# A hybrid decoder layer: the first feed-forward product, nine feature groups token-major, with seven products for eight in half of their k

## The chip, the cores and the metric

The kernel runs on one core of one Trainium2 chip. The metric is device time of one execution in microseconds (us). The core has five instruction streams: TensorE (PE; its weight loads are listed as PEld), VectorE (DVE), ScalarE (ACT), GpSimd (POOL) and SyncE (SP), which issues the loads. Each engine takes its instructions in the order in which the program emits them and waits at those whose inputs or buffers aren't ready.

## The reference

One post-norm decoder layer over 256 tokens, D = 2048: a token-mixing part (attention, a gated MLP over tokens, a state-space branch, gates and an output product) and a feed-forward part of width D_FF = 5632. What the change touches is the feed-forward part:

```python
x = _layer_norm(ALPHA * x + merged @ w_o[l], ln1_g[l], ln1_b[l]).astype(dt)
gate_f, up = jnp.split(x @ w_ffn_in[l], 2, axis=-1)
f = (jax.nn.silu(gate_f) * up) @ w_ffn_out[l]
x = _layer_norm(ALPHA * x + f, ln2_g[l], ln2_b[l]).astype(dt)
```

## The kernel before

**Numbers in two parts.** Every product is made from float32 values split in two: a high part (the value rounded by the type fp32r, `split_h`, line 254, on ScalarE) and the remainder (value minus high part, `split_l`, line 265, on VectorE; both of its inputs lie in SBUF). A product a.b is taken as ah.bh + al.bh + ah.bl.

**Units.** The whole program is a list of units. A unit is one weight tile of up to 128 x 1024 values (512 KB): it is loaded into a `raw` tile (4 buffers), split into `wh` and `wl` (4 buffers each), and used by its matmuls. The main loop (line 1210) goes through the units in order. `advance` emits the loads and the splits of high parts ahead of the unit that is due, as far as the four buffers allow; `remainders` emits split_l after the unit's `post`, so the order of VectorE's work is: what `post` does, then the remainders of the units to come. `top_up` (line 285) emits a load when fewer than four raw tiles are loaded and not yet split. All loads go through SP's one queue.

**The first product, x @ w_ffn_in.** It has 88 feature tiles of 128: for each f of 44 a gate tile and an up tile, alternating (`f1`, line 1137). The first four go through `quad_tiles`, beside the end of the layer norm; the other 84 through `wide` (line 83). There the weights are stationary and the 256 tokens stream: `wide_mm` (line 74) takes for each of 16 k-tiles one matmul of 512 columns on line 79 (high part of the weights by high and low part of the activations, `x1T`, which holds [high | low] of the tokens, feature-major) and one of 256 columns on line 80 (remainder of the weights by the high part). A tile takes two units. `post_f1` (line 1040) adds the two halves of the PSUM bank, takes tanh of the gate, multiplies, and splits the product into `h_tile(f)`: h0 (tag x24) holds f 0 to 11, and eleven tiles of tag s6 hold three f each. h is the second product's activation, again feature-major.

**The second product, h @ w_ffn_out.** `tall` and `tall_mm` (lines 169 and 159) work the other way: a token tile's activations (128 x 128) are stationary and 512 output features stream, three matmuls for each k-tile and token tile on lines 165 to 167. The result is token-major. w_v, w_zv and w_o are made in this way too; w_o's activations, the tiles m, are of tag s6.

**Memory.** Tiles of one tag share a fixed number of buffers, laid out one tag after the other. The large tags are t32 (x1T), t16 (z, the residual stream after the first layer norm, until the second), raw, wh, wl, x24, s6 (11 buffers of 1536 values per partition) and the temporaries. After the constants, and between x24 and s6, stand small tiles whose sizes aren't multiples of 1 KB; one of them is `s5i`, 96 bytes, ahead of s6. PSUM has four banks of tag mm and four of tag sd.

**Elsewhere on GpSimd.** It runs the state-space recurrence (lines 544 to 547, 48 values a partition) in the first half of the program, adds gated branches (line 868) and a part of the layer norms (lines 937 and 938). In the first feed-forward product it does nothing.

Of the kernel before, what the change touches and what calls it, by code (L numbers as in the profile page):

```python
# [25 lines left out]
NJ = 24  # L26
# [6 lines left out]
def hybrid_layer(ctx: ExitStack, tc: tile.TileContext, d: dict, out: bass.AP):  # L33
# [5 lines left out]
    V, A, G, T = nc.vector, nc.scalar, nc.gpsimd, nc.tensor  # L39

    RAW_BUFS, HL_BUFS, AHEAD = 4, 4, 4

    def bank(tag="mm"):
        return psp.tile([128, 512], F32, tag=tag, bufs=4, name=f"ps_{tag}")

    def tmp(n=512):

        if n <= 256:
            t = sb.tile([128, 256], F32, tag="t1", bufs=6, name="tmp1")
        else:  # L50
            t = sb.tile([128, 512], F32, tag="t2", bufs=6, name="tmp2")
        return t[:, :n]

    def s6(shape, dt, name):
        return sb.tile(shape, dt, tag="s6", bufs=11, name=name)

    def copy_split(hi, lo, src, scale=1.0):
        A.activation(hi, src, AF.Copy, scale=scale)  # L58
        if scale == 1.0:
            V.tensor_tensor(lo, src, hi.bitcast(F32), op=ALU.subtract)  # L60
        else:
            V.scalar_tensor_tensor(lo, src, scale, hi.bitcast(F32), op0=ALU.mult, op1=ALU.subtract)


    class Unit:
        def __init__(self, src, k, n, mm, post=None, before=None, uses=1, home=None, fence=False):
            self.src, self.k, self.n = src, k, n
            self.mm, self.post, self.before = mm, post, before
            self.uses, self.home, self.fence = uses, home, fence

# [134 lines left out]
    def spawn(gen, rate=1, first=False):  # L205

        tasks.append((gen, rate, first))
        return gen
# [12 lines left out]
    def later(fn, wait=1):  # L221

        deferred.append([fn, wait])
# [16 lines left out]
    with tc.manual_schedule():  # L240
# [4 lines left out]
        def raw_tile():  # L245
            return sb.tile([128, 1024], F32, tag="raw", bufs=RAW_BUFS, name="raw")

        def load(n):
            u = units[n]
            r = raw_tile()  # L250
            nc.sync.dma_start(r[:, :u.k * u.n], u.src)
            raws[n] = r

        def split_h(n):
            u = units[n]
            m = u.k * u.n
# [5 lines left out]
            A.activation(h[:, :m], raws[n][:, :m], AF.Copy)  # L262
            hl[n] = rest[n] = (h, l)

        def split_l(n):
            m = units[n].k * units[n].n
            h, l = rest.pop(n)
            V.tensor_tensor(l[:, :m], raws.pop(n)[:, :m], h[:, :m].bitcast(F32), op=ALU.subtract)  # L268

        pos = {}  # L270

# [106 lines left out]

        def s5_setup():
            P = s5["P"]  # L380
            PI = sb.tile([128, NJ], I32, tag="s5i", bufs=1, name="s5i")
# [639 lines left out]
        def h_tile(f):  # L1021
            if f < 12:
                if f == 0:
                    big["h0"] = sb.tile([128, 12, 512], F32R, tag="x24", bufs=1, name="h0")
                return big["h0"][:, f, :]
            i = (f - 12) // 3
            if (f - 12) % 3 == 0 and ("h", i) not in big:
                big["h", i] = s6([128, 3, 512], F32R, f"h{i}")
            return big["h", i][:, (f - 12) % 3, :]

# [9 lines left out]
        def post_f1(f, up):  # L1040
# [11 lines left out]
                    copy_split(y[:, 0:256], y[:, 256:512], w, 0.5)  # L1052
            return post

        def post_f2(g):
# [19 lines left out]
        def ln2_load():  # L1075
            w = sb.tile([128, 2, D], F32, tag="t32", bufs=1, name="ln2w")
# [67 lines left out]
        for srcs, post in f1[4:]:  # L1144
            wide(srcs, 8, act_x1, post)
# [60 lines left out]
        pos.update(load=4, h=4, l=4, live=4, seq=seq)  # L1206
        while top_up():
            pass
        marks["s5"] = spawn(s5_setup())
# [140 lines left out]
```

## Time and profile before

| | us |
|---|---|
| median of 3 runs | 1604.29 (1601.53 to 1605.39) |
| the profiled execution | 1604.32 |
| its span, first to last instruction | 1602.6 |
| TensorE busy | 1580.8 (99%) |
| VectorE busy | 931.0 (58%) |
| ScalarE busy | 763.8 (48%) |
| GpSimd busy | 559.9 (35%) |
| mean granted TensorE clock | 0.995 |

The busy times are sums over the whole span. TensorE's matmuls are pipelined, so one instruction's listed duration is longer than the distance to the next; the work of a stretch is read from the number of matmuls in a window and its length. A line of a timeline gives start, duration, engine, line and operation, out<-in, shapes; a number in brackets at its end is idle time before it and what ended that.

### The profile page before, as it was taken

The numbers are of one execution on the slowest core, as the hardware profiler recorded it, in microseconds if no ns is written. First come the engines' busy times: TensorE is split into PE (matmuls) and PEld (weight loads), VectorE is DVE, ScalarE is ACT, GpSimd is POOL, SyncE is SP. The second block draws the span as 40 slices with busy tenths as digits, with TensorE's granted clock in tenths as the row PEclk, the third lists the DMA queues.
The fourth block names the chain that finished last, engine by engine and source line by source line (L and its number), as shares of the span: only waits on it lengthen the run. The fifth ranks groups of instructions, "written<-read, shape, count | busy, mean of one in ns | idle before, by whom it ended". The sixth has DMA issues, their size and how long they took to land.

```text
span 1602.6 us, 24113 instructions
## 1 busy us (share of the span) xinstructions
PE 1580.8 (99%) x9094; PEld 1366.3 (85%) x9094; DVE 931.0 (58%) x1232; ACT 763.8 (48%) x1040; POOL 559.9 (35%) x1147
## 2 busy tenths in 40 slices
PE   8999999999999999999999999999999999999996
PEld 7888888898999998889789888888888888888885
DVE  5444555556855565469667556565555555445455
ACT  5444434456544444475444545554444544333342
POOL 7569999933999999203011000000000000000002
PEclk9999999999999999999999999999999999999998
DMA  8575557655656555557863565555555556666663
GB/s 275 176 251 186 187 203 207 155 148 188 211 188 198 194 184 194 178 164 209 286 222 118 190 193 184 184 184 184 186 185 192 183 193 237 204 187 192 186 188 101
DMA packets 106492, 307.50 MB, mean 192 GB/s; under 512 B 27567, under 2 KB 28079, under 8 KB 106120
## 3 DMA queue, kind: packets, MB, share of 16 engines
q1 hardware_dynamic: 106280, 305.82, 59.7%
q8 instruction: 71, 1.16, 0.3%
q14 instruction: 45, 0.37, 0.1%
q0 software_dynamic: 96, 0.15, 0.0%
HBM read 303.78 MB, written 5.53 MB: 193 GB/s over the span
## 4 chain that ended last, share of the span: by engine, by line
PE 94%; DVE 3%; DMA 1%; ACT 1%; issue 0%; POOL 0%; SPq 0%; POOLq 0%; ACTq 0%
PE ps_mm L79 40%; PE ps_mm L80 20%; PE ps_mm L165 9%; PE ps_mm L166 9%; PE ps_mm L167 9%; DVE wl L268 1%; PE ps_mm L857 1%; PE ps_mm L858 1%; PE ps_mm L856 1%; PE ps_sd L522 1%; PE ps_sd L691 1%; PE ps_mm L108 0%; PE ps_mm L111 0%; PE ps_sd L670 0%; DMA ln<-in_ln_g_dram 0%
## 5 line engine op out<-in xcount | busy, mean ns | idle before, releaser
L268 DVE TENSOR_TENSOR wl<-raw,wh 128x1024 fp32r<-128x1024 f32 (+1 forms) x544 | 654.2, 1227 | 167.1 <-ACT wh L262 166.6
L262 ACT ACTIVATE wh<-raw 128x1024 fp32r<-128x1024 f32 (+1 forms) x544 | 556.7, 1024 | 369.1 <-PE ps_mm L167 171.6
L79 PE MATMUL ps_mm<-xT,wh 128*128 128x512 f32 x1344 | 480.6, 400 | 6.6 <-ACT wh L58 5.9
L79 PE MATMUL ps_mm<-x1T,wh 128*128 128x512 f32 x1344 | 474.9, 399 | 0.0
L80 PE MATMUL ps_mm<-xT,wl 128*128 128x256 f32 x1344 | 378.9, 282 | 0.5 <-DVE wl L268 0.5
L80 PE MATMUL ps_mm<-x1T,wl 128*128 128x256 f32 x1344 | 377.5, 281 | 0.0
L79 PEld LDWEIGHTS ps_mm<-xT,wh 128*128 128x128 f32 x1344 | 254.3, 189 | 67.1 <-ACT wh L58 5.9
L79 PEld LDWEIGHTS ps_mm<-x1T,wh 128*128 128x128 f32 x1344 | 252.6, 188 | 63.0
L937 POOL TENSOR_TENSOR z<-z,ln2w 128x512 f32<-128x512 f32 (+1 forms) x4 | 5.2, 1302 | 732.5 <-ACT z L936 732.5
L80 PEld LDWEIGHTS ps_mm<-xT,wl 128*128 128x128 f32 x1344 | 256.1, 191 | 1.5 <-DVE wl L268 0.8
L80 PEld LDWEIGHTS ps_mm<-x1T,wl 128*128 128x128 f32 x1344 | 253.9, 189 | 0.0
L546 POOL TENSOR_TENSOR X<-X,t 128x48 f32<-128x48 f32 x255 | 129.1, 506 | 48.6 <-ACT X L526 48.6
L544 POOL TENSOR_TENSOR t<-s5keep,X 128x48 f32<-128x48 f32 x254 | 126.6, 498 | 44.5 <-ACT X L526 24.7
L547 POOL TENSOR_TENSOR X<-X,t 128x48 f32<-128x48 f32 x255 | 129.9, 509 | 20.0
L166 PE MATMUL ps_mm<-wl,h 128*128 128x512 f32 x340 | 134.1, 394 | 0.0
L165 PE MATMUL ps_mm<-wh,h 128*128 128x512 f32 x340 | 134.1, 394 | 0.0
L167 PE MATMUL ps_mm<-wh,h 128*128 128x512 f32 x340 | 134.1, 394 | 0.0
L1037 DVE TENSOR_TENSOR tmp<-ps_mm,tmp 128x256 f32<-128x256 f32 x88 | 37.3, 424 | 152.9 <-ACT tmp L1036 152.9
L545 POOL TENSOR_TENSOR t<-s5keep,X 128x48 f32<-128x48 f32 x254 | 108.5, 427 | 0.0
L315 ACT ACTIVATE tmp<-ps_mm,bcol 128x256 f32<-128x256 f32 x90 | 42.7, 474 | 137.6 <-PE ps_mm L80 137.4
L1036 ACT ACTIVATE tmp<-ps_mm 128x256 f32<-128x256 f32 x88 | 33.8, 384 | 151.6 <-PE ps_mm L80 151.6
L165 PEld LDWEIGHTS ps_mm<-wh,h 128*128 128x128 f32 x340 | 64.0, 188 | 15.0
(214 smaller groups left out, 1775.6 us busy)
## 6 DMA issues: line engine op xcount, KB each, us to landing
raw<-in_w_f_dram SPq DMA_DIRECT2D x264, 512.0 KB, 4.3
raw<-in_w_b_dram SPq DMA_DIRECT2D x164, 512.0 KB, 4.6
raw<-in_w_o_dram SPq DMA_DIRECT2D x32, 512.0 KB, 5.0
raw<-in_w_v_dram SPq DMA_DIRECT2D x24, 512.0 KB, 4.0
raw<-in_w_p_dram SPq DMA_DIRECT2D x32, 384.0 KB, 3.4
raw<-in_w_zv_dram SPq DMA_DIRECT2D x16, 384.0 KB, 3.6
tmp<-tab SPq DMA_DIRECT2D x64, 64.0 KB, 3.2
raw<-in_w_p_dram SPq DMA_DIRECT2D x16, 256.0 KB, 2.9
```

The lines of the kernel that those rows point to most:

```text
L79: T.matmul(ps, lhsT=h[:, j * 128:(j + 1) * 128], rhs=a, start=k == 0, stop=last, skip_group_check=True)
L80: T.matmul(ps[:, 0:256], lhsT=l[:, j * 128:(j + 1) * 128], rhs=a[:, 0:256], start=False, stop=last, skip_group_check=True)
L165: T.matmul(ps[:, :n], lhsT=ah, rhs=hs, start=k == 0, stop=False)
L166: T.matmul(ps[:, :n], lhsT=ah, rhs=ls, start=False, stop=False)
L167: T.matmul(ps[:, :n], lhsT=al, rhs=hs, start=False, stop=k == total - 1)
L262: A.activation(h[:, :m], raws[n][:, :m], AF.Copy)
L268: V.tensor_tensor(l[:, :m], raws.pop(n)[:, :m], h[:, :m].bitcast(F32), op=ALU.subtract)
L315: A.activation(t, ps[:, 256:512], AF.Identity, bias=bcol[:, col:col + 1], scale=scale)
L544: G.tensor_tensor(t1, keep[:, 0], prev, op=ALU.mult)
L545: G.tensor_tensor(t2, keep[:, 1], prev[:, :, ::-1], op=ALU.mult)
L546: G.tensor_tensor(cur, cur, t1, op=ALU.add)
L547: G.tensor_tensor(cur, cur, t2, op=ALU.add)
```

## The change

1. **Groups.** The first 8 feature tiles (f 0 and 1 in the quad, f 2 and 3 wide) and the last 8 (f 40 to 43) stay as they were. The 72 tiles between become nine groups (`seven(g)`, g = 1 to 9) of four f, gate and up: per group two matrices of 512 columns, gate (`g`) and up (`u`). They are made token-major, like the second product: three matmuls of 512 columns for each k-tile, token tile and matrix (`three`).
2. **Seven products for eight.** For k-tiles 0 to 7, taken in pairs (SP = 4 steps), the 2 x 2 blocks (token tile by k-tile, k-tile by gate/up) are multiplied by Strassen's scheme in Winograd's form. The weights' combinations are made by GpSimd in `combine`, four subtractions or additions of 128 x 512 a step; one is made in place in the `u` tile before its split. Each step has four units: `g` and `u` (1024 values a partition), `t1` (512) and `tt` (1024); t1 and tt have no load and are split like the others. The activations' combinations are made once (`sums`: ten GpSimd operations) and split into `S`. For k-tiles 8 to 15 a group has eight plain units of 1024, two for each pair of k-tiles, that go on in the same PSUM banks.
3. **Results.** `evict` (after step 4) copies four PSUM banks on ScalarE and combines them on GpSimd (four operations of 128 x 512); `gates_` and `ups` add the other four banks on VectorE (one input in PSUM), take tanh and multiply (four operations with both inputs in SBUF, in `rest`). The result is token-major; `turns(g)` turns it with eight transposes of 128 x 128 during the next group and splits it into h.
4. **Loads.** A weight tile now takes two k-tiles of four feature tiles, so that its source is in pieces of 1 KB where it was 4 KB a partition. `g` tiles live in tag s6, three ahead (two in the last group); `top_up` counts raw and `g` tiles apart.
5. **z** goes to DRAM before the groups and comes back at the second product, since `S` takes its place (t16).
6. **Addresses.** `s5i` moves to the constants and 320 bytes of padding follow it; all large tiles then start at multiples of 1 KB.

```diff
+    PAD = 80
+    SP = 4
+    FIRST, LAST = 1, 9
...
         def load(n):
             u = units[n]
-            r = raw_tile()
-            nc.sync.dma_start(r[:, :u.k * u.n], u.src)
+            if u.role in ("t1", "tt"):
+                return
+            if u.role == "g":
+                r = u.pair["g"] = s6([128, 1536], F32, "gt")
+                pos["g"] += 1
+            else:
+                r = raw_tile()
+                pos["raw"] += 1
...
+            if u.role == "g":
+                combine(u.pair)
+            elif u.role == "t1":
+                raws[n] = u.pair["g"][:, 1024:1536]
+            elif u.role == "tt":
+                raws[n] = u.pair["t"]
             A.activation(h[:, :m], raws[n][:, :m], AF.Copy)
...
+        def combine(p):
+            p["t"] = s6([128, 1024], F32, "tt")
+            b = [p[e][:, 0:1024].rearrange("p (f k c) -> p k f c", f=4, k=2) for e in "gu"]
+            b11, b21, b12, b22 = b[0][:, 0], b[0][:, 1], b[1][:, 0], b[1][:, 1]
...
+            G.tensor_tensor(t1, b12, b11, op=ALU.subtract)
+            G.tensor_tensor(b12, b22, b12, op=ALU.subtract)
+            G.tensor_tensor(t2, b12, b11, op=ALU.add)
+            G.tensor_tensor(t4, b21, t2, op=ALU.subtract)
...
         def top_up():
             seq = pos["seq"]
-            if pos["load"] < len(seq) and pos["load"] - pos["l"] < RAW_BUFS:
+            if pos["load"] < len(seq):
+                u = units[seq[pos["load"]][0]]
+                if u.role == "g" and pos["g"] >= u.pair["ahead"] or u.role in (None, "u") and pos["raw"] >= RAW_BUFS:
+                    return False
...
+        s5["i"] = const.tile([128, NJ], I32, name="s5i")
+        const.tile([128, PAD], F32, name="pad")
...
+        def first_sums():
+            big["zd"] = dram.tile([128, 2, D], F32, name="zd")
+            for t in range(2):
+                nc.sync.dma_start(big["zd"][:, t, :], big["z"][:, t, :])
+            spawn(sums())
...
+        def three(ps, a, h, l, start, stop):
+            T.matmul(ps, lhsT=a[0], rhs=h, start=start, stop=False)
+            T.matmul(ps, lhsT=a[1], rhs=h, start=False, stop=False)
+            T.matmul(ps, lhsT=a[0], rhs=l, start=False, stop=stop)
...
+                    if role == "g":
+                        prod(1, act2(0, 2 * i), cols(h, 0), cols(l, 0), i)
+                        prod(2, act2(0, 2 * i + 1), cols(h, 1), cols(l, 1), i)
+                    elif role == "u":
+                        prod(7, act_s(2, i), cols(h, 0), cols(l, 0), i)
+                        prod(3, act_s(3, i), cols(h, 1), cols(l, 1), i)
+                    elif role == "t1":
+                        prod(5, act_s(0, i), h[:, 0:512], l[:, 0:512], i)
+                    else:
+                        prod(6, act_s(1, i), h[:, 0:512], l[:, 0:512], i)
+                        prod(4, act2(1, 2 * i + 1), h[:, 512:1024], l[:, 512:1024], i)
...
+            def evict():
+                c = P["c"] = {n: tmp() for n in (1, 7, 5, 6)}
+                for n in (1, 7, 5, 6):
+                    A.activation(c[n], P[n], AF.Copy)
+                G.tensor_tensor(c[6], c[1], c[6], op=ALU.add)
+                G.tensor_tensor(c[7], c[6], c[7], op=ALU.add)
+                G.tensor_tensor(c[6], c[6], c[5], op=ALU.add)
+                G.tensor_tensor(c[5], c[7], c[5], op=ALU.add)
...
+            def ups():
+                c = P["c"]
+                for n, m in ((6, 3), (5, 8)):
+                    V.tensor_tensor(c[n], P[m], c[n], op=ALU.add)
+                def rest(t):
+                    w, a, b = P["w"][t], c[(1, 7)[t]], c[(6, 5)[t]]
+                    V.scalar_tensor_tensor(w, w, 1.0, a, op0=ALU.add, op1=ALU.mult)
+                    V.tensor_tensor(w, w, b, op=ALU.mult)
...
+            src = [d["w_f1"][8 * g + up:8 * g + 8:2].rearrange("f p k c -> p f k c") for up in range(2)]
...
+        for g in range(FIRST, LAST + 1):
+            seven(g)
```

More of the change, by code (lines that the diff above doesn't have):

```diff
@@ L380, in s5_setup @@
             P = s5["P"]
-            PI = sb.tile([128, NJ], I32, tag="s5i", bufs=1, name="s5i")
+            PI = s5["i"]
             keep = const.tile([128, 3, NJ, 2], F32, name="s5keep")
@@ L1026, in h_tile @@
             i = (f - 12) // 3
-            if (f - 12) % 3 == 0 and ("h", i) not in big:
+            if ("h", i) not in big:
                 big["h", i] = s6([128, 3, 512], F32R, f"h{i}")
@@ L1053, in post_f1, with sums @@
             return post
+        def first_sums():
[3 more added lines that the diff above has]
+            spawn(sums())
+        def sums():
+            srs = []
+            for j in range(SP // 2):
+                xr = s6([128, 4, 256], F32, "xr")
+                x = big["x1T"][:, 4 * j:4 * j + 4, :].bitcast(F32)
+                G.tensor_tensor(xr, x[:, :, 0:256], x[:, :, 256:512], op=ALU.add)
+                sr = s6([128, 4, 2, 128], F32, "sr")
+                a = xr.rearrange("p (i k) (t c) -> p k t i c", k=2, t=2)
+                a11, a21, a12, a22 = a[:, 0, 0], a[:, 0, 1], a[:, 1, 0], a[:, 1, 1]
+                G.tensor_tensor(sr[:, 0], a21, a22, op=ALU.add)
+                G.tensor_tensor(sr[:, 1], sr[:, 0], a11, op=ALU.subtract)
+                G.tensor_tensor(sr[:, 2], a11, a21, op=ALU.subtract)
+                G.tensor_tensor(sr[:, 3], a12, sr[:, 1], op=ALU.subtract)
+                srs.append(sr)
+            for _ in range(3):
+                yield
+            big["S"] = sb.tile([128, 4, SP, 256], F32R, tag="t16", bufs=1, name="S")
+            for j in range(SP // 2):
+                o = big["S"][:, :, 2 * j:2 * j + 2, :]
+                for s in range(4):
+                    copy_split(o[:, s, :, 0:128], o[:, s, :, 128:256], srs[j][:, s])
+                    if s % 2:
+                        yield
@@ new lines, in seven, with cols, prod, mk @@
+        def seven(g):
+            P = {}
+            def cols(w, j):
+                return w.rearrange("p (f k c) -> p k f c", f=4, k=2)[:, j]
+            def prod(n, a, h, l, i):
+                if i == 0 and n not in P:
+                    P[n] = bank("sd" if n in (1, 5, 6, 7) else "mm")
+                three(P[n], a, h, l, i == 0, n in (1, 5, 6, 7) and i == SP - 1)
+            def mk(role, i):
+                def mm(h, l):
+                    if role == "g":
[9 more added lines that the diff above has]
+                        prod(4, act2(1, 2 * i + 1), h[:, 512:1024], l[:, 512:1024], i)
+                return mm
+            def mk8(up, i):
+                def mm(h, l):
+                    for t in range(2):
+                        n = ((2, 4), (3, 8))[up][t]
+                        if n == 8 and i == SP:
+                            P[8] = bank("mm")
+                        for j in range(2):
+                            three(P[n], act2(t, 2 * i + j), cols(h, j), cols(l, j),
+                                  n == 8 and (i, j) == (SP, 0), (i, j) == (7, 1))
+                return mm
+            def begin():
+                if g > FIRST:
+                    spawn(turns(g - 1))
+            def evict():
[6 more added lines that the diff above has]
+                G.tensor_tensor(c[5], c[7], c[5], op=ALU.add)
+            def gates_():
+                c = P["c"]
+                for n, m in ((1, 2), (7, 4)):
+                    V.tensor_tensor(c[n], P[m], c[n], op=ALU.add)
+                P["w"] = [tmp(), tmp()]
+                for t, n in enumerate((1, 7)):
+                    A.activation(P["w"][t], c[n], AF.Tanh, scale=0.5)
+            def ups():
+                c = P["c"]
+                for n, m in ((6, 3), (5, 8)):
+                    V.tensor_tensor(c[n], P[m], c[n], op=ALU.add)
+                def rest(t):
+                    w, a, b = P["w"][t], c[(1, 7)[t]], c[(6, 5)[t]]
+                    V.scalar_tensor_tensor(w, w, 1.0, a, op0=ALU.add, op1=ALU.mult)
+                    V.tensor_tensor(w, w, b, op=ALU.mult)
+                rest(0)
+                later(lambda: rest(1), 0)
+                big["w", g] = P["w"]
+            src = [d["w_f1"][8 * g + up:8 * g + 8:2].rearrange("f p k c -> p f k c") for up in range(2)]
+            for i in range(8):
+                s = [a[:, :, 2 * i:2 * i + 2, :].rearrange("p f k c -> p f (k c)") for a in src]
+                if i < SP:
+                    pair = {"ahead": 3 if g < 9 else 2}
+                    units.append(Unit(s[0], 8, 128, mk("g", i), role="g", pair=pair,
+                                      before=begin if i == 0 else None))
+                    units.append(Unit(s[1], 8, 128, mk("u", i), role="u", pair=pair))
+                    units.append(Unit(None, 4, 128, mk("t1", i), role="t1", pair=pair))
+                    units.append(Unit(None, 8, 128, mk("tt", i), role="tt", pair=pair,
+                                      post=evict if i == SP - 1 else None))
+                else:
+                    units.append(Unit(s[0], 8, 128, mk8(0, i), post=gates_ if i == 7 else None))
+                    units.append(Unit(s[1], 8, 128, mk8(1, i), post=ups if i == 7 else None))
@@ new lines, in turns @@
+        def turns(g):
+            tag = "mm" if g < LAST else "sd"
+            for _ in range(6 if g < LAST else 2):
+                yield
+            for t in range(2):
+                ps = bank(tag)
+                for f in range(4):
+                    T.transpose(ps[:, f * 128:(f + 1) * 128], big["w", g][t][:, f * 128:(f + 1) * 128], ident)
+                yield
+                f = 4 * g
+                while f < 4 * g + 4:
+                    n = min(4 * g + 4, 12 if f < 12 else f + 3 - f % 3) - f
+                    h_tile(f)
+                    y = big["h0"][:, f:f + n] if f < 12 else big["h", (f - 12) // 3][:, f % 3:f % 3 + n]
+                    copy_split(y[:, :, t * 128:(t + 1) * 128], y[:, :, 256 + t * 128:256 + (t + 1) * 128],
+                               ps.rearrange("p (f c) -> p f c", f=4)[:, f - 4 * g:f - 4 * g + n], 0.5)
+                    f += n
+                for _ in range(3 if g < LAST else 1):
+                    yield
@@ L1075, in ln2_load @@
         def ln2_load():
+            big["z"] = sb.tile([128, 2, D], F32, tag="t16", bufs=1, name="z")
+            for t in range(2):
+                nc.sync.dma_start(big["z"][:, t, :], big["zd"][:, t, :])
             w = sb.tile([128, 2, D], F32, tag="t32", bufs=1, name="ln2w")
@@ L1205, in hybrid_layer @@
             seq.insert(at + i, (first + i, at))
[L1206 removed]
+        pos.update(load=4, h=4, l=4, live=4, raw=0, g=0, seq=seq)
         while top_up():
```

34 lines of the change are left out of this document (30 added, 4 removed).

## The prediction

> **What bounds the kernel now.** I read the page first (busy times, then the chain that ended last), then a table by windows of the stretch that the change rewrites: the first feed-forward product after its quad, 84 feature tiles on lines 79 and 80. Columns of the window row: TensorE, its weight loads, VectorE, ScalarE, GpSimd, granted clock, DMA share, GB/s.
>
> ```profile
> PE 1580.8 (99%) x9094; PEld 1366.3 (85%) x9094; DVE 931.0 (58%) x1232; ACT 763.8 (48%) x1040; POOL 559.9 (35%) x1147
> ...
> PE 94%; DVE 3%; DMA 1%; ACT 1%; issue 0%; POOL 0%; SPq 0%; POOLq 0%; ACTq 0%
> ```
>
> ```profile
> 868.70:1343.30 474.60, 474.60 (x2689) 411.62 (x2688) 282.26 (x382) 238.17 (x340) 0.00 (x0) 1.00 0.58 187
> ```
>
> TensorE never stops there, at full clock; VectorE works 59% of the time, ScalarE 50%, GpSimd not at all. So TensorE sets the time: 474.6 / 84 = 5.65 us a tile, 45.2 us for the eight tiles of one group, 407 us for the nine groups. All sums below stand against the profiled execution, 1604.3 us (span 1602.6 and 1.7 around it), which is also the median.
>
> **TensorE's part.** The new form (a token tile's activations as weights, 512 weight columns streaming, three products) is that of the second product, lines 165 to 167. Two windows of its second pass, TensorE alone:
>
> ```profile
> 1404.93:1421.28 16.35, 16.35 (x73) 1.00 0.60 191
> 1421.28:1466.25 44.97, 44.97 (x193) 1.00 0.64 188
> ```
>
> The windows start and end on a product, so they hold 72 and 192: 0.227 and 0.234 us each. The 72 read h0, which starts at the same offset within 1 KB as the weight tiles; the 192 read tiles of tag s6, 96 bytes (the integer tile s5i) further on. The change puts all of them at multiples of 1 KB, so I take 0.227 for the groups and keep 0.234 as the other end. A group has 4 steps of seven products and 4 of eight, 60 triples, 180 instructions: 40.9 us (42.1). Turning the result back costs two sets of four transposes; one set is this row, at most 0.60:
>
> ```profile
> 839.53 0.60 PE L956 MATMUL ps_sd<-ident,z 128*128 128x128 f32 x4
> ```
>
> TensorE's group is then 42.1 us (43.3) for 45.2: 3.1 us saved, 28 us in nine groups, if TensorE still sets the time. Outside the groups, 32 of 44 k-tiles of the second product and all of w_o read s6 tiles: 768 + 384 products. If w_o's run like the 192, 0.007 us each give 8 us (0 if offsets don't matter).
>
> **What is added on the other engines.** Per group: ScalarE makes 20 high parts of 1024 and 4 of 512 where it made 16; by the 1058 ns of the row below and half of it, 23.3 us, and eight operations of 512 for the results, 4.2 us more: far below 42. VectorE makes as many remainders (split_l), GpSimd gets 16 combinations and 4 additions of 128x512. These two I price together, because the trace shows them waiting for each other:
>
> ```profile
> L268 DVE TENSOR_TENSOR wl<-raw,wh 128x1024 fp32r<-128x1024 f32 x474 | 583.9, 1255 | 163.2 <-ACT wh L262 162.7
> L262 ACT ACTIVATE wh<-raw 128x1024 fp32r<-128x1024 f32 x474 | 501.2, 1058 | 357.4 <-PE ps_mm L167 171.6 <-PE ps_mm L79 79.1 <-DMA raw<-in_w_o_dram 28.2
> ```
>
> ```profile
> 200.90 1.17 POOL L544 TENSOR_TENSOR t<-s5keep,X 128x48 f32<-128x48 f32 x1
> 202.03 0.31 POOL L545 TENSOR_TENSOR t<-s5keep,X 128x48 f32<-128x48 f32 x1
> ```
>
> ```profile
> 200.60 1.29 DVE L268 TENSOR_TENSOR wl<-raw,wh 128x1024 fp32r<-128x1024 f32 x1 [1.31 <-ACT wh L262]
> ```
>
> ```profile
> 841.26 1.28 POOL L938 TENSOR_TENSOR z<-z,ln 128x512 f32<-128x512 f32 x1
> ...
> 851.39 1.28 POOL L937 TENSOR_TENSOR z<-z,ln 128x512 f32<-128x512 f32 x1 [0.58 <-ACT z L936]
> 852.75 2.14 POOL L938 TENSOR_TENSOR z<-z,ln 128x512 f32<-128x512 f32 x1
> ```
>
> ```profile
> 851.88 4.09 DVE L268 TENSOR_TENSOR wl<-raw,wh 128x1024 fp32r<-128x1024 f32 x2
> 855.89 0.68 DVE L60 TENSOR_TENSOR x1T<-ps_sd,x1T 128x512 fp32r<-128x512 f32 x1
> 856.49 1.21 DVE L268 TENSOR_TENSOR wl<-raw,wh 128x1024 fp32r<-128x1024 f32 x1
> 857.63 0.69 DVE L60 TENSOR_TENSOR x1T<-ps_sd,x1T 128x512 fp32r<-128x512 f32 x1
> ```
>
> A GpSimd step of 0.31 us takes 1.17 while a remainder runs. At 851.88 two remainders take 4.09 us, where one alone takes 1.14 (856.49 to the next start): the first waits for GpSimd's end at 852.67, GpSimd's next (alone 1.28) then lasts until 854.89, and the second remainder ends at 855.97. They run strictly in turn: 1.15 us for GpSimd's 512, 1.08 for VectorE's 1024. An operation that reads one input from PSUM is not held:
>
> ```profile
> 838.30 1.62 POOL L938 TENSOR_TENSOR z<-z,ln 128x512 f32<-128x512 f32 x1
> ...
> 838.97 0.69 DVE L60 TENSOR_TENSOR x1T<-ps_sd,x1T 128x512 fp32r<-128x512 f32 x1 [0.20 <-ACT x1T L58]
> ```
>
> The Trainium skill ("SBUF — State Buffer", Who interferes with whom) says that a VectorE instruction with two SBUF inputs and a GpSimd instruction that reads SBUF exclude each other for the whole instruction. That speaks against this change and the trace agrees; whole instructions (20 x 1.22, 8 x 0.69, 20 x 1.28) would add up to 55.5 us a group where my rows, which allow for the ends that overlap, give the following.
>
> In turn, per group: 20 remainders of 1024 at 1.08 = 21.6; 4 of 512 and the 4 two-input steps of `rest`, 0.55 each (half), = 4.4; GpSimd 20 x 1.15 = 23.0. Sum **49.0 us**, above TensorE's 42.1 and above the 45.2 of before. No order of issue makes a group shorter than this.
>
> It will be longer, since the work is not spread evenly. How soon loads land (KB each, median us from issue to landing), here and for the copies below:
>
> ```profile
> raw<-in_w_f_dram SPq DMA_DIRECT2D x264, 512.0 KB, 4.3
> ...
> out_dram<-z SPq DMA_DIRECT2D x14, 128.0 KB, 2.3
> ...
> ln2w<-in_ln_g_dram SPq DMA_DIRECT2D x1, 1024.0 KB, 5.8
> ...
> out_dram<-z SPq DMA_DIRECT2D x4, 64.0 KB, 2.0
> ```
>
> Second half of a group (plain units): TensorE needs 96 x 0.227 = 21.8 us, VectorE only 8 remainders, so TensorE sets it. GpSimd can't use it fully: a `u` tile takes a raw buffer that split_l of about the fifth plain unit frees, and the copy lands some 4.3 us later, about 11 us into the half. In the other 11 us it does some six of the sixteen combinations. First half of the next group: VectorE has 2 PSUM sums of `ups` at 0.60, then `rest` (4 x 0.55), and only behind these, on its queue, the remainders of t1 and tt on which TensorE waits; in all 10 x 1.08 + 4 x 0.55 + 2.2 + 1.2, and 1.2 for the turned h: 17.6 us. Ten GpSimd operations fall between them, 11.5 us, and TensorE's last two products end 1.4 us later: 30.5 us. A group is 21.8 + 30.5 = **52.3 us**, 7.1 more than before.
>
> The same thing stops TensorE already today, around 720, where each unit has a GpSimd sum of 256:
>
> ```profile
> 718.54 0.95 DVE L268 TENSOR_TENSOR wl<-raw,wh 128x768 fp32r<-128x768 f32 x1
> ...
> 721.04 1.50 DVE L268 TENSOR_TENSOR wl<-raw,wh 128x768 fp32r<-128x768 f32 x1
> ```
>
> ```profile
> 720.87 0.85 POOL L868 TENSOR_TENSOR mab<-mab,g 128x256 f32<-128x256 f32 x1 [0.77 <-DVE g L866]
> ```
>
> ```profile
> by line: DVE wl L268 52.9%; DVE m L60 15.7%; PE ps_mm L858 10.7%; PE ps_mm L857 10.6%; PE ps_mm L856 9.0%; issue 8.9%; DVE g L866 3.8%
> ```
>
> The remainder of 768 waits for GpSimd's end at 721.72 (0.95 us becomes 1.50), and remainders hold 53% of the chain from 718 to 726.
>
> Further waits: ScalarE's split of `u` waits for GpSimd's second combination, with the splits of t1 and tt and the four eviction copies behind it; that is inside the 30.5. On SP the fourth `g` load waits for the first tt remainder, and behind it stand the fourth `u` and the plain loads, which aren't due for 15 us.
>
> Costed at nothing: the sums of x1T (some 14 us of GpSimd, 5 of VectorE) beside the quad and four wide tiles (22.6 us), where GpSimd is idle; uncovered, 5 to 10 us. z to DRAM and back: two copies of 1 MB each way, at the 5.8 us of the 1 MB row; SP's lead of four raw and four split tiles (over 20 us) hides them; uncovered, 12 us. The loads in pieces of 1 KB for 4 KB: of the rows above, the 64 KB stores go in rows of 1 KB and the 128 KB ones in rows of 2 KB; no collapse there, but they are small. DMA stands at a share of 0.58, so a load could cost half as much again (0.87) before DMA set the time. I take 0, with up to 2 us a group (20 us) kept for the top of the range.
>
> **Sum.** Eight groups at +7.1 = +57; the first group has no predecessor to evict, about +1; offsets outside -8. 1604.3 + 50 = **1654 us**. At the floor of 49.0 a group: 9 x 3.8 - 8 = +26, 1630.
>
> **Rivals.**
> - *TensorE still sets the time* (faster). GpSimd's combination holds VectorE up for less than 1.15 us, or GpSimd gets so far ahead that only idle time is used. Decides: 26.0 of VectorE plus 20 h must stay under 42.1, so h under 0.80 us. Then 1604.3 - 28 - 8 = 1568 (0.234: 1584). For it: GpSimd is free today, VectorE 41% idle. Against it: the rows at 851.88 are not an average, they show the whole wait. Chance 0.09.
> - *Half way*: the waits fall mostly into VectorE's gaps, a group comes to 44 to 47: 1588 to 1615, say 1600. Chance 0.05.
> - *Alignment quickens every product* (faster, or less slow): if the part of a product that doesn't grow with its columns vanished. Window of w_zv, 384 columns (the first and last are cut; 15 whole ones in 2.60 us, 0.173):
>
> ```profile
> 316.53:319.15 2.62, 2.62 (x17) 1.00 0.64 175
> ```
>
> (0.227 - 0.173) / 128 gives 0.42 ns a column, so 0.215 for 512 and 0.323 for a wide pair that takes 0.353 now. By the code 84 + 12 wide tiles of 16 pairs remain, 1,536: -46; 1,728 token-major products of 512 outside the groups at 12 ns: -21; 1654 - 67 = 1587. Against it: equal offsets already exist (0.227), and the wide pairs have them and still take 0.353. Chance 0.03. The Trainium skill ("TensorE: Matmul & The Clock Gate", Back-to-back issue gap) gives N/2.4 + 2.5 ns, 216 ns for 512; no run here shows a product of these that fast.
> - *Starved as well* (slower still): the fourth pair's load waits for a buffer, the 1 KB copies land late, and no combination is done ahead: six more GpSimd operations in the first half, 59 us a group: 1604.3 + 9 x 14 - 8 = 1722. Chance 0.05 for above 1700.
>
> **How the numbers follow.** The forecast, both engines in turn, has 0.78. Its own range goes from the floor, 1630, to 1654 with 20 us for the pieces of 1 KB and 12 for the uncovered copies, 1686. Widened at the bottom into the half-way case and at the top toward the starved one it is 1600 to 1700; outside lie 0.09 + 0.03 + half of 0.05 below and 0.05 above, 0.2. A measurement of this kernel tells 0.3% (4.8 us) from no change. Faster: 0.09 + 0.03 and half of the half-way case, 0.15; same 0.02; slower 0.83.
>
> **What would show it.** Right: in the groups, TensorE's busy share falls to about 80%, its idle time ends on VectorE's wl, mostly for the t1 and tt units; GpSimd's combinations average over 2 us where 1.28 is theirs alone, and VectorE's remainders well over 1.25; second halves run at 21.8 us, first halves near 30. Wrong: combinations at 1.3 us beside remainders at 1.2, or product pitches under 0.22 us. The lines 165 to 167 should read 0.227 throughout; if they stay at 0.234, the 8 us are gone.

## The result, and the profile after

The changed kernel takes 1689.97 us (median of 4 runs, 1689.23 to 1690.83) against 1603.78 for the kernel before on the same chip: ratio 1.054, interval 1.052 to 1.0557. It is 86 us slower; the forecast was 1654, slower by 50, with a range of 1600 to 1700. The profiled execution spans 1688.4 us, 85.8 more than the one of before.

The page of the changed kernel: busy times, the granted clock in forty slices of 42 us, and the chain of work that ended last.

```profile
PE 1591.4 (94%) x8482; PEld 1337.7 (79%) x8482; DVE 1116.4 (66%) x1236; ACT 806.7 (48%) x1062; POOL 899.8 (53%) x1337
...
PEclk9999999999999999999997899888989999999998
...
PE 81%; DVE 12%; DMA 2%; ACT 2%; issue 2%; POOL 0%; SPq 0%; DVEq 0%; POOLq 0%; ACTq 0%
```

TensorE's instructions fell from 9094 to 8482, but its busy time did not (1580.8 to 1591.4 us); in the longer span its share is 94% for 99%. VectorE's share of the chain rose from 3% to 12%. Now the stretches of the change, in the table by windows (columns as in the prediction: TensorE, its weight loads, VectorE, ScalarE, GpSimd, granted clock, DMA share, GB/s): the nine groups, the two halves of the fourth group, the four wide tiles ahead of the groups, then the second and the first pass of the second product.

```profile
897.91:1384.44 486.53, 418.97 (x1687) 322.08 (x1686) 416.79 (x320) 243.85 (x302) 317.56 (x175) 0.92 0.49 153
...
1057.94:1090.66 32.72, 25.47 (x94) 18.21 (x92) 31.84 (x26) 15.38 (x21) 23.83 (x13) 0.84 0.24 75
1090.66:1112.42 21.76, 21.76 (x97) 18.02 (x96) 15.99 (x13) 11.54 (x15) 15.29 (x9) 1.00 0.89 290
...
866.66:897.90 31.24, 24.52 (x130) 20.78 (x129) 19.75 (x26) 13.90 (x27) 9.60 (x8) 0.89 0.81 263
...
1495.06:1554.89 59.83, 59.83 (x265) 49.55 (x264) 29.48 (x27) 23.35 (x22) 0.00 (x0) 1.00 0.62 194
1430.54:1495.06 64.52, 62.05 (x267) 50.62 (x266) 29.09 (x27) 24.02 (x24) 0.00 (x0) 0.97 0.73 254
```

The groups take 486.5 us where nine groups of tiles took 406.8: +79.7. The halves differ as forecast: in the second (plain units) TensorE never stops, 21.8 us; in the first (the Strassen steps) VectorE works 31.84 of 32.72 us, and TensorE stands for over a fifth of it. The wide tiles ahead of the groups take 31.2 us for 22.6: +8.6. The second product gains 1.3 us, the stretch from w_o to the wide tiles 4.0, and 2.8 are lost in small shifts elsewhere: together the 85.8 us between the spans.

What the groups wait for. First four groups of instructions from 925 to 1360 us, shapes apart (count, then busy us, mean ns), then two rows of the waits in the groups (us in total, times, longest), for TensorE's weight loads and for its matmuls:

```profile
L304 DVE TENSOR_TENSOR wl<-gt,wh 128x1024 fp32r<-128x1024 f32 x32 | 61.7, 1929 | 9.6 <-ACT wh L284 9.6
L298 POOL TENSOR_TENSOR tt<-gt,tt 128x512 f32<-128x512 f32 x32 | 61.3, 1915 | 2.5
...
L304 DVE TENSOR_TENSOR wl<-tt,wh 128x1024 fp32r<-128x1024 f32 x32 | 55.3, 1727 | 0.5 <-ACT wh L284 0.2
...
L1215 DVE TENSOR_TENSOR tmp<-tmp,tmp 128x512 f32<-128x512 f32 x16 | 24.5, 1532 | 0.6
```

```profile
PEld ps_sd L1145 <- DVE wl L304: 99.1, 71, 6.4
...
PE ps_sd L1145 <- DVE wl L304: 66.7, 52, 6.0
```

A remainder of 1024 that takes 1.22 us alone takes 1.7 to 1.9, the combination shown 1.9 for 1.28, a step of `rest` 1.5 for 0.69. TensorE's matmuls stand 67.6 us in the groups (486.53 less 418.97), and 66.7 of these end on VectorE's remainder. How they hold each other is seen in the order of time, from the first half of the fourth group, VectorE first (start, duration), then GpSimd:

```profile
1066.19 2.30 DVE L304 TENSOR_TENSOR wl<-tt,wh 128x1024 fp32r<-128x1024 f32 x1
1068.41 2.30 DVE L304 TENSOR_TENSOR wl<-gt,wh 128x1024 fp32r<-128x1024 f32 x1
1070.63 2.30 DVE L304 TENSOR_TENSOR wl<-raw,wh 128x1024 fp32r<-128x1024 f32 x1
```

```profile
1067.49 2.14 POOL L296 TENSOR_TENSOR raw<-raw 128x512 f32<-128x512 f32 x1
1069.71 2.14 POOL L297 TENSOR_TENSOR tt<-raw,gt 128x512 f32<-128x512 f32 x1
1071.93 2.15 POOL L298 TENSOR_TENSOR tt<-gt,tt 128x512 f32<-128x512 f32 x1
```

Both engines start an instruction every 2.22 us: one remainder and one combination in each period, each standing while the other runs. The prediction's prices, 1.08 and 1.15, add up to 2.23.

### The profile page after: what moved, and what is told of

The parts are those of the page before. It is cut to its first block, busy times and chain, and to the rows that moved or that the text cites. A ratio compares the mean times of both kernels' runs of the same rounds, so it can differ in the third digit from the quotient of the medians.

```text
span 1688.4 us, 23448 instructions
## 1 busy us (share of the span) xinstructions
PE 1591.4 (94%) x8482; PEld 1337.7 (79%) x8482; DVE 1116.4 (66%) x1236; ACT 806.7 (48%) x1062; POOL 899.8 (53%) x1337
## 3 DMA queue, kind: packets, MB, share of 16 engines
q8 instruction: 66, 1.08, 0.3%
## 4 chain that ended last, share of the span: by engine, by line
PE 81%; DVE 12%; DMA 2%; ACT 2%; issue 2%; POOL 0%; SPq 0%; DVEq 0%; POOLq 0%; ACTq 0%
PE ps_mm L84 21%; PE ps_mm L85 11%; PE ps_mm L170 8%; PE ps_mm L171 8%; PE ps_mm L172 8%; DVE wl L304 8%; PE ps_mm L1143 4%; PE ps_mm L1145 4%; PE ps_mm L1144 4%; PE ps_mm L905 2%; PE ps_mm L904 2%; PE ps_mm L903 2%; PE ps_sd L1145 1%; DMA raw<-in_w_f_dram 1%; DVE tmp L1214 1%
## 5 line engine op out<-in xcount | busy, mean ns | idle before, releaser
L304 DVE TENSOR_TENSOR wl<-raw,wh 128x1024 fp32r<-128x1024 f32 (+2 forms) x508 | 656.3, 1309 | 194.7 <-ACT wh L284 191.8
L284 ACT ACTIVATE wh<-raw 128x1024 fp32r<-128x1024 f32 (+2 forms) x508 | 517.6, 1023 | 434.9 <-PE ps_mm L172 164.2
L591 POOL TENSOR_TENSOR t<-s5keep,X 128x48 f32<-128x48 f32 x254 | 124.5, 490 | 44.5 <-ACT X L573 24.7
L1143 PE MATMUL ps_mm<-wh,x1T 128*128 128x512 f32 x360 | 144.2, 401 | 0.0
L593 POOL TENSOR_TENSOR X<-X,t 128x48 f32<-128x48 f32 x255 | 118.2, 464 | 47.8 <-ACT X L573 47.8
L1144 PE MATMUL ps_mm<-wh,x1T 128*128 128x512 f32 x360 | 143.7, 399 | 0.0
L1145 PE MATMUL ps_mm<-wl,x1T 128*128 128x512 f32 x360 | 143.5, 399 | 0.0
L594 POOL TENSOR_TENSOR X<-X,t 128x48 f32<-128x48 f32 x255 | 128.4, 503 | 20.0
L592 POOL TENSOR_TENSOR t<-s5keep,X 128x48 f32<-128x48 f32 x254 | 122.5, 482 | 0.0
L304 DVE TENSOR_TENSOR wl<-gt,wh 128x1024 fp32r<-128x1024 f32 x72 | 109.4, 1520 | 9.6 <-ACT wh L284 9.6
L1145 PE MATMUL ps_sd<-wl,S 128*128 128x512 f32 x108 | 53.8, 498 | 59.1 <-DVE wl L304 58.3
L295 POOL TENSOR_TENSOR gt<-raw,gt 128x512 f32<-128x512 f32 x36 | 63.7, 1769 | 56.6 <-DMA raw<-in_w_f_dram 48.0
L1145 PEld LDWEIGHTS ps_sd<-wl,S 128*128 128x128 f32 x108 | 22.5, 208 | 88.2 <-DVE wl L304 85.9
```

Source lines behind the costliest of these rows:

```text
L591: G.tensor_tensor(t1, keep[:, 0], prev, op=ALU.mult)
L594: G.tensor_tensor(cur, cur, t2, op=ALU.add)
L1143: T.matmul(ps, lhsT=a[0], rhs=h, start=start, stop=False)
L1144: T.matmul(ps, lhsT=a[1], rhs=h, start=False, stop=False)
L1145: T.matmul(ps, lhsT=a[0], rhs=l, start=False, stop=stop)
```

## Experiments

Theory: in turn. GpSimd's combinations and VectorE's operations with two inputs in SBUF run one after the other, and where they stand thick VectorE's remainders come too late for TensorE. Rivals: the loads in pieces of 1 KB; the order on VectorE's queue; VectorE's own load. All times below are medians against about 1602.5 us of the kernel before, on the same chip; windows are of the nine groups.

**1. The four combinations become fills that read nothing**

```
-G.tensor_tensor(t1, b12, b11, op=ALU.subtract)
...
+for o in (t1, b12, t2, t4):
+    G.memset(o, 0.0)
```

> The four combinations of each step are replaced by four write-only fills of the same tiles on GpSimd: same count, same places, same queue, same waits for the loads, but nothing is read (the weight combinations are left out). Theory 'in turn' (GpSimd operations that read SBUF and VectorE remainders run one after the other): the first halves fall from 32 us to TensorE's 20 to 23, a group to 42 to 45 us, the kernel to 1590 to 1610 us; remainders of 1024 back to 1.1 to 1.3 us. Rival 'late loads' (1 KB pieces): the loads and the waits for them are the same, so groups stay near 54 us and the kernel near 1685. Rival 'VectorE's queue' (rest and the PSUM sums stand ahead of the t1 and tt remainders): groups come down only by the shorter GpSimd work, to 50 or more, 1655 or more. If a write-only fill holds VectorE as well, the groups come down by the fill's shorter duration only.

Measured: 1591.82 us, ratio 0.9931 (0.9916 to 0.9946). The groups' window, and then the fill and a remainder by their source lines (nanoseconds min/median/max, first and last start):

```profile
897.69:1286.19 388.50, 380.04 (x1687) 308.97 (x1685) 309.57 (x314) 245.50 (x300) 134.20 (x169) 1.00 0.61 191
```

```profile
L296 POOL MEMSET tt<- x72: 523/527/533, 890.7 to 1256.9; 128x512 f32 x72
```

```profile
L302 DVE TENSOR_TENSOR wl<-tt,wh x36: 1212/1220/1227, 900.6 to 1261.5; 128x1024 fp32r<-128x1024 f32 x36
```

98 us of the groups are gone: 43.2 us a group. A fill reads nothing, and it is also shorter, 0.53 us for 1.28. But the fills didn't merely cost less: no remainder of tt took over 1.227 us and no fill over 0.533, so neither held the other at all. The loads, the queue and the places are those of the change; pieces of 1 KB and the order on VectorE's queue alone can't be what cost the 80 us.

**2. Copies with one input instead**

```
+for o, i in ((t1, b12), (b12, b22), (t2, b11), (t4, b21)):
+    G.tensor_copy(o, i)
```

> The four combinations of each step become four copies of one input each on GpSimd, same tiles, places and waits (the weight combinations are left out). Theory 'a GpSimd operation that reads SBUF excludes a two-input VectorE operation, however many inputs it reads': remainders of t1, tt and g stay stretched, and a group comes down only by the shorter operations, 46 to 53 us, kernel 1615 to 1680. Rival 'only a two-input GpSimd operation holds VectorE': as with the fills, 43.4 a group and 1592.

Measured: 1613.62 us, ratio 1.0069 (1.0054 to 1.0084); the groups 412.6 us, 45.8 each.

```profile
L296 POOL COPY tt<-gt x72: 608/804/3822, 891.1 to 1281.9; 128x512 f32<-128x512 f32 x72
```

A copy takes 0.61 us alone, about a fill's time, but its median is 0.80 and many wait far longer, as the fills never do: one input in SBUF is enough to be held. Between experiments 1 and 2 the length is nearly the same and reading is the difference: 24 us of the 98. The other 74 go with the length of a combination, 1.28 us for 0.61. The kernel ends just under the lower end of what was expected, as I had not known how short a copy is. VectorE was also held less than expected: the median remainder of tt stays at 1.22 us, the longest is 1.63.

**3. The combinations on VectorE**

```
-G.tensor_tensor(t1, b12, b11, op=ALU.subtract)
...
+V.tensor_tensor(t1, b12, b11, op=ALU.subtract)
...
```

> The 16 combinations of a group move from GpSimd to VectorE, the busier engine; the four additions of the eviction stay on GpSimd. Theory 'in turn': an operation of 512 costs 0.55 to 0.69 us on VectorE alone, and 1.15 in turn on GpSimd, so the sum of the two engines falls from 49.0 to 26.0 + 16 x 0.6 + 4 x 1.15 = 40 us a group, with 4 us of PSUM work beside it on VectorE: 44 to 48 us a group, kernel 1605 to 1640, faster than the change although VectorE gets more work. Rival 'no exclusion, VectorE's own load or order': 16 more operations on the engine that TensorE waits for add some 10 us to the first half, 60 us a group or more, kernel above 1740. Rival 'late loads': VectorE now itself waits for the loads of u, with the remainders behind: no faster than the change, 1690 or more.

Measured: 1661.04 us, ratio 1.0363 (1.0349 to 1.0377): 29 us faster than the change though the engine that TensorE waits for got 16 operations more a group, but 21 us above the upper end of what was expected. First half of the fifth group:

```profile
1098.80:1128.90 30.10, 24.53 (x93) 18.36 (x92) 28.63 (x37) 16.02 (x21) 0.00 (x0) 0.89 0.24 70
```

VectorE is busy 28.63 of 30.10 us with GpSimd idle. So moving the work ends the holding, not the thick place: the first half is bound by VectorE's own work. My sum was made for the whole group, as if the second half's idle time could be used.

**4. Token-major without Strassen**

Eight products of eight in all of k (`SP = 0`), gates straight from PSUM, no copy of z.

> The nine groups token-major with eight products of eight in all of k: no combinations, no sums of x1T, no copy of z to DRAM and back, gates straight from PSUM; the loads in 1 KB pieces and the offsets at multiples of 1 KB stay. 192 products at 0.227 and 1.2 of transposes give 44.8 us a group, 403 for nine (407 before); with the offsets w_o -4 and the second product -5: 1590 to 1596 us. Rival 'late loads' (pieces of 1 KB make the loads late or slow VectorE and ScalarE): TensorE waits in the groups here too, 1610 or more.

Measured: 1591.16 us, ratio 0.9927 (0.9914 to 0.9941), as expected.

```profile
890.74:1290.37 399.63, 399.63 (x1794) 330.71 (x1793) 209.82 (x210) 173.01 (x193) 0.00 (x0) 1.00 0.62 191
```

TensorE never stops, with the same 1 KB pieces: 44.4 us a group. Token-major was no loss; the seven products for eight, where the change puts them, were.

**5. The offsets alone, in the kernel before**

```
+s5["i"] = const.tile([128, NJ], I32, name="s5i")
+const.tile([128, 80], F32, name="pad")
...
-PI = sb.tile([128, NJ], I32, tag="s5i", bufs=1, name="s5i")
+PI = s5["i"]
```

> The kernel before with the one part of the change that moves the s6 tiles to multiples of 1 KB. Theory (a product whose operands stand at equal offsets within 1 KB takes 0.227 us for 0.234): w_o -4, 768 products of the second feed-forward product -5, together 1594 to 1596 us. Rival (offsets don't matter, w_o's gain in the change has another cause): 1604.

Measured: 1597.57 us, ratio 0.9966 (0.9953 to 0.9978): 5 us, and 1.6 us above the range that was expected. The second pass of the second product, before (first row, the kernel before) and with the offsets:

```profile
1404.93:1466.25 61.32, 61.32 (x265) 49.68 (x264) 29.51 (x27) 23.34 (x22) 0.00 (x0) 1.00 0.63 189
```

```profile
1403.40:1463.23 59.83, 59.83 (x266) 49.56 (x265) 29.48 (x27) 23.34 (x22) 0.00 (x0) 1.00 0.64 194
```

1.5 us a pass, 6 in four, and 2.7 in w_o (92.1 to 89.4); w_o itself starts 2.6 us later than before, for a reason that these runs don't show.

**6. `rest` behind the remainders of the next group**

```
-rest(0)
-later(lambda: rest(1), 0)
+later(lambda: rest(0), 3)
+later(lambda: rest(1), 5)
```

> The changed kernel with the two halves of rest issued three and five units later, so that on VectorE's queue the remainders of the next group's first four units stand ahead of them. Theory 'in turn' (what bounds a group is the sum of both engines' whole operations, 20 x 1.22 + 4 x 0.68 + 4 x 0.69 on VectorE and 20 x 1.22 on GpSimd, 54 us): the sum stays, so a group stays within 1.5 us of 54, the kernel at 1676 to 1700. Rival 'VectorE's order': TensorE no longer waits for rest ahead of t1 and tt, some 4 to 6 us less a group, 1635 to 1655.

Measured: 1699.75 us, ratio 1.0606 (1.0587 to 1.0625); 490.5 us of groups for 486.5. In the full change the order is worth nothing; the rival falls here.

**7. The eviction's additions on VectorE, from PSUM**

```
-for n in (1, 7, 5, 6):
-    A.activation(c[n], P[n], AF.Copy)
-G.tensor_tensor(c[6], c[1], c[6], op=ALU.add)
...
+A.activation(c[1], P[1], AF.Copy)
+for o, n, x in ((6, 6, 1), (7, 7, 6), (6, 5, 6), (5, 5, 7)):
+    V.tensor_tensor(c[o], P[n], c[x], op=ALU.add)
```

> The changed kernel; the four additions of the eviction go from GpSimd (behind four copies by ScalarE) to VectorE, each with one input in PSUM (behind one copy). Theory 'in turn' with 'PSUM inputs are not held': the sum in turn falls by 4 x 1.22 us, 54 to 49 a group, and 4 x 0.69 of VectorE lie beside GpSimd's work; what is seen of it depends on whether GpSimd uses the time it gains for the next combinations: 49 to 53 a group, kernel 1645 to 1682. Rival 'VectorE's own load': VectorE gets 2.8 us a group more and the groups get longer, 1690 to 1715.

Measured: 1696.0 us, ratio 1.0582 (1.0566 to 1.0598): a miss, and a number in the rival's range; the groups take 491.5 us for 486.5. 4.9 us a group less in turn, and nothing came of it. The first combination of a pair in this kernel: what GpSimd waited for (us, times).

```profile
  DMA raw<-in_w_f_dram: 217.5, 9
```

The additions lie in the second half, where TensorE sets the time (21.8 us in every group here too). GpSimd could have used the time only for the next group's combinations, but it stands some 24 us a group (217.5 / 9) until the load of `u` has landed. So a sum over the whole group is not the measure. Whether the 5 us more are VectorE's 2.8 us a group of additions, as the rival has it, stays open.

**8. The copies of z to DRAM earlier**

```
 elif (t, q, e) == (1, 1, 0):
     turn(1, 2)
+    spill(0)
...
 elif (t, q, e) == (1, 1, 3):
     turn(1, 3)
+    spill(1)
```

> The changed kernel with the two copies of z to DRAM issued while the quad still runs, ahead of the loads behind which they stood on SP's queue (issued at 875 us, z complete at 853). Theory: the 8.6 us that the four wide tiles lost is ScalarE's wait for this copy; the tiles take 22.6 to 24 us again, the groups stay, kernel 1680 to 1684. Rival (the split of the sums and GpSimd's sums cost the same without the wait, or the copy delays the loads instead): 1687 to 1692.

Measured: 1681.94 us, ratio 1.0497 (1.048 to 1.0515). The four wide tiles in this kernel:

```profile
868.52:891.13 22.61, 22.61 (x131) 19.64 (x129) 18.70 (x28) 14.86 (x28) 5.73 (x6) 1.00 0.83 275
```

The 8.6 us are gone, and the groups stay at 485.3. In the changed kernel, SP's queue, GpSimd's, and who waited for the copy:

```profile
875.29 1.29 SPq L1106 DMA_DIRECT2D zd<-z  x2
```

```profile
850.68 2.15 POOL L985 TENSOR_TENSOR z<-z,ln 128x512 f32<-128x512 f32 x1
```

```profile
  ACT S L61: 7.8, 1
```

z was complete at 852.8 us, the copy issued at 875.3, behind loads on SP's queue that had to wait for buffers, and ScalarE stood 7.8 us at the split of the sums, with the next tiles' high parts behind it.

**9 and 10. Two steps of seven products instead of four**

`SP = 2`: on GpSimd as in the change (two_steps), and with combinations and additions on VectorE (two_steps_vector). In both the result of the group before is also turned earlier in the group than in the change.

> Seven products for eight in a quarter of k instead of half (two steps of eight), combinations on GpSimd as in the change; the split of the sums starts three units later and z comes back before the last wide tiles. Theory 'in turn': VectorE 18 x 1.22 + 2 x 0.68 + 4 x 0.69 = 26.1, GpSimd (8 + 4) x 1.22 = 14.6, together 40.7 us a group, less than TensorE's 186 x 0.227 + 1.2 = 43.4: TensorE sets the time again, 43.4 to 46 a group, kernel 1578 to 1604, faster than before. Rival 'any GpSimd work beside the remainders costs its full length' (13 us of it a group on top of the token-major group of 44): 50 a group or more, above 1630.

> As two_steps, but with the eight combinations and the four additions on VectorE (the additions with one input in PSUM): GpSimd idle in the groups. VectorE per group 18 x 1.22 + 2 x 0.68 + (4 + 8) x 0.69 + 8 x 0.69 + 4 x 0.7 = 40 us, TensorE 43.4: TensorE sets the time, 43 to 45 a group, kernel 1575 to 1592, the fastest of all if the plain token-major form (1591) is beaten. Rival: VectorE at 92% is late at the start of each group, where its work is thickest: 46 to 48, 1600 to 1615.

Measured: 1626.15 us, ratio 1.0148 (1.0133 to 1.0163), and 1641.31 us, ratio 1.0241 (1.0225 to 1.0256): both missed. The sums, 41 us in turn and 40 on VectorE alone, are less than TensorE's 43.4, and still a group takes 48.6 and 49.9 (the rivals had 50 or more, and 46 to 48). VectorE in two_steps at the start of the fourth group, then TensorE's wait:

```profile
1038.40 1.27 DVE L1210 TENSOR_TENSOR tmp<-ps_mm,tmp 128x512 f32<-128x512 f32 x2
1039.60 0.68 DVE L1214 SCALAR_TENSOR_TENSOR tmp<-tmp,tmp 128x512 f32<-128x512 f32 x1
1040.31 1.67 DVE L1215 TENSOR_TENSOR tmp<-tmp,tmp 128x512 f32<-128x512 f32 x1
1041.90 1.75 DVE L1214 SCALAR_TENSOR_TENSOR tmp<-tmp,tmp 128x512 f32<-128x512 f32 x1
1043.69 0.69 DVE L1215 TENSOR_TENSOR tmp<-tmp,tmp 128x512 f32<-128x512 f32 x1
1044.30 0.68 DVE L304 TENSOR_TENSOR wl<-gt,wh 128x512 fp32r<-128x512 f32 x1
```

```profile
1045.04 0.79 PE L1145 MATMUL ps_sd<-wl,S 128*128 128x512 f32 x1 [3.10 <-DVE wl L304]
```

The remainder that TensorE stood for 3.1 us stands behind the previous group's sums and its rest, two of them stretched by combinations. The two steps took 15 us there, where TensorE needs 42 x 0.227 and the turning, 10.7; the other six steps ran at TensorE's pace. In two_steps_vector nothing stands in turn any more, but the place is the same. The first two steps of its sixth group:

```profile
1138.49:1156.81 18.32, 13.85 (x52) 10.39 (x50) 15.93 (x22) 9.58 (x13) 0.00 (x0) 0.81 0.26 72
```

VectorE's own combinations stand there ahead of a remainder for which TensorE waits 2.25 us, and the clock is 0.81.

**11. Two steps, `rest` later, z copied early**

> As two_steps (combinations on GpSimd), with rest issued two and four units later, and z copied to DRAM while the quad still runs. Theory 'in turn, but only where work stands thick': in two_steps the sum, 41 us a group, is under TensorE's, and what TensorE waits for at each group's start is the t1 remainder behind ups and rest on VectorE's queue, 4.6 us of the chain; behind the remainders rest costs nothing, so a group goes from 47.7 to 43.4 to 45, and the first from 54 to 46 by the early copy: kernel 1580 to 1600. Rival 'the sum in turn alone, at any place' (rest_later on the full change moved nothing): groups stay at 47 to 48, 1616 to 1626.

(The turning also starts two units later than in two_steps.) Measured: 1617.13 us, ratio 1.0093 (1.0078 to 1.0108); 47.3 us a group. The rival's number, not mine. First two steps of the fifth group:

```profile
1076.32:1091.03 14.71, 10.99 (x52) 8.45 (x50) 14.18 (x16) 8.94 (x12) 4.73 (x3) 1.00 0.23 71
```

VectorE is busy 14.18 of 14.71 us: once `rest` had moved back, the remainders, sums and turned h that were left still filled the place, and `rest` fell among them.

**12. Two steps, spread**

```
-for i in range(8):
+for i in (2, 3, 4, 0, 5, 1, 6, 7):
```

with the additions of experiment 7, the early copy of experiment 8, and z fetched back before the last wide tiles.

> Two steps of seven products as in two_steps, but at the fourth and sixth place of a group's eight steps instead of the first two, away from ups, rest and the turned h; the eviction's additions on VectorE with one input in PSUM, the combinations on GpSimd, the early copy of z. Theory 'what counts is how thick the work in turn stands, place by place': per group VectorE 18 x 1.22 + 2 x 0.68 + 4 x 0.69 + 12 x 0.7 of PSUM work = 34.5 and GpSimd 8 x 1.22 = 9.8 that may lie beside the PSUM work; over the first ten units it stands at 19 to 23 us for TensorE's 22, then 12 for 10 and 9 for 11, so TensorE sets the time nearly everywhere: 43.4 to 45 a group (two_steps 48.5, two_steps_rest_later 47.3), kernel 1582 to 1598. Rival 'the number of combinations counts, not their place': 47 to 48 a group, 1615 to 1625.

Measured: 1580.97 us, ratio 0.9865 (0.9849 to 0.9882): faster than the kernel before by 21.8 us, than the change by 109 and than the plain token-major form by 10, the best of all and 1 us under the expected range. The groups' window, and one of the combinations:

```profile
888.68:1278.94 390.26, 389.15 (x1741) 320.01 (x1739) 322.05 (x314) 206.05 (x237) 130.95 (x72) 1.00 0.63 195
```

```profile
L298 POOL TENSOR_TENSOR tt<-gt,tt 128x512 f32<-128x512 f32 x16 | 34.5, 2158 | 1.3
```

43.4 us a group, the sum of TensorE's own products, and TensorE stands 1.1 us in 390. The combinations are as slow as ever (the one shown 2.16 us for 1.28): the holding is still there, but each stretch now has room for it. Beside the order, three things differ from experiment 11: the additions, `rest` (issued as in the change) and the PSUM banks in which the result is turned. The additions, moved alone, brought nothing in experiment 7, moving `rest` brought nothing in experiment 6, and with the combinations on VectorE (experiment 10) the groups were longer, so the place of the eight combinations is the likelier cause of 43.4 for 47.3; the order by itself was not run.

## Why the prediction was right, and where it was off

- **Which engine sets the time**: right. "They run strictly in turn" is what the rows at 1066 us show, at 2.22 us a pair for 2.23. Experiment 1 takes away the reading and with it over half of each operation's length, and 98 us go; reading alone, at nearly the same length, costs 24 (experiments 1 and 2). The Trainium skill ("SBUF — State Buffer", Who interferes with whom) lets a GpSimd instruction that only writes go free of this; experiment 1 agrees, with 0.527 us a fill beside unstretched remainders.
- **Second half 21.8**: right to the tenth (21.76).
- **First half 30.5**: mis-sized, 32.3 in the mean of groups 2 to 9. The term at fault is the ten GpSimd operations: ten combinations start in the first halves of groups 2 and 3 (31.0 and 31.2 us), 11 or 12 in those of groups 4 to 9 (32.5 to 33.1). At the start of a group three to five of its sixteen were done, not six; the reason given, the load of `u`, holds. One or two more at 1.15 us are most of the missing 1.7. Eight groups make 54.0 - 45.2 = 8.8 each, 70 us for 57.
- **First group "about +1"**: wrong, 54.4 us for 46. "No predecessor to evict" was true and didn't help. It isn't the copy of z: with experiment 8 it took 55.1; with combinations that read nothing (experiment 1) the first group takes 41.3. The trace has the splits of the sums of x1T at its start: two of them take 2.91 us between combinations (at 901.58 us), 0.76 without (at 888.20), and the last wide tile's results stand there too. VectorE is busy 31.59 of the first 32.64 us. The prediction had put these splits beside the wide tiles. A run without them was not made.
- **Costed at nothing**: the copies of z (uncovered: 12) cost 8.6, and this is the step that failed outright. I let SP's lead hide them; the issue stood behind waiting loads on SP's queue. On the way back they cost again: the first pass of the second product takes 64.5 us for 59.8, as z stands ahead of the weights on SP's queue; in experiment 12, with z fetched earlier, that pass takes 59.9. The 1 KB pieces cost nothing (experiment 4).
- **Offsets -8**: the products came right, 59.83 us a pass at 0.227; done alone, the offsets are worth 5 us.
- **Sum**: forecast +57 +1 -8 = +50. Measured 79.7 in the groups (70.5 and 9.2), 8.6 in the wide tiles, and -2.5 for the rest, 85.8. The 36 us between them: 13.5 from the first halves, 8 from the first group, 8.6 from the copy and 5.5 from outside these stretches. There the products at equal offsets gave some 10 (4.0 from w_o to the wide tiles, 6.0 in the second product), but z's way back took 4.7 and small shifts 2.8.
- **The range**: it holds 1690 partly by luck. The forecast's own range ended at 1686, and 20 us of that were kept for the pieces of 1 KB, which cost nothing; the first halves and the first group, which had no allowance, filled the place.
- **What would show it**: TensorE's share in the groups is 86% (419.0 of 486.5) for about 80; combinations average 1.7 to 1.9 us, short of the 2 that were named, remainders 1.6 to 1.9; of TensorE's 67.6 us idle, 52 are before the products of t1 and tt, as said.
- **Rivals**: "TensorE still sets the time" was priced at 1568, with h under 0.80 us as its point; the fills (no holding) give 1592, with 43.2 us a group for its 42.1 and the losses around z. (Its other number, 1584 for 0.234, should be 1587: nine groups at 1.9 us less are 17 us.) "Half way", "alignment quickens every product" (TensorE at 0.227 a product wherever it doesn't wait) and "starved as well" didn't come. The floor of 49.0 a group was no forecast, and no kernel with all sixteen combinations on GpSimd came near it; experiments 7, 9 and 11 show that a sum over a group promises too much.

## What to carry to other kernels

Before work is given to an idle GpSimd, ask whether VectorE reads two SBUF operands at that place: here the two engines then worked as one, 2.22 us a pair. Price it where it stands, half by half, not over the loop: with eight combinations a group took 47.3 us where they stood next to the end of the previous group and 43.4 where they stood between plain steps (kernels that differ in more than the place). And look at what the new transfers stand behind on their queue, not only at how long they take.

## What the runs showed that I had not expected

TensorE's clock fell after waits. After the wait of 3.10 us in two_steps the next products take 0.43 us each, then 0.23 (two windows, clock in the third column from the end):

```profile
1045.10:1048.30 3.20, 3.20 (x10) 2.63 (x11) 3.20 (x3) 1.10 (x2) 0.00 (x0) 0.50 0.00 0
1048.70:1051.70 3.00, 3.00 (x16) 2.48 (x16) 2.33 (x5) 2.67 (x4) 0.00 (x0) 1.00 0.54 157
```

So a wait may cost about 1 us more than itself (an estimate: five products at 0.2 us each). In the first half of the change's fourth group the mean clock is 0.84, and there it cost next to nothing: VectorE is busy 31.84 of 32.72 us, and after the slow products TensorE waited for remainders again (0.23 us at 1076.92, 0.57 at 1079.15). The Trainium skill ("TensorE: Matmul & The Clock Gate", The HAM clock gate) has this half rate, after an idle window of about 3.4 us. Here shorter waits were enough: 3.1 us in two_steps, 2.25 us in experiment 3, where the clock is 0.50 from 1071.8 to 1075.0.
